# One more empty step between loading the spatial weights and using them, in a fused diffusion-transformer layer

## Chip, cores and metric

The kernel runs on one core of one Trainium2 chip. The time is device microseconds (us) of one execution; the median of several runs counts.

## The reference

One layer over 2048 latent tokens (model width 1024) and 256 context tokens, all in float32. The part that matters here is the token-mixing half: one combined input projection, whose columns are keys, values, queries, the gMLP's u and v, and two gates, then attention and the gMLP, merged by the gates.

```python
h_x = modulate(x, norm1_g[l], sh1, sc1)
p_x = h_x @ w_in[l]
...
q_x, u_x, vg_x, ga_x, gb_x = jnp.split(p_x[..., KV_COLS:], REST_SPLITS, axis=-1)
...
gm_x = gmlp_spatial(jax.nn.gelu(u_x), jax.nn.gelu(vg_x), gm_norm_g[l], gm_ws[l], gm_bs[l])

def gmlp_spatial(u, v, gm_norm_g, gm_ws, gm_bs):
    ...
    vg = rmsnorm(v.reshape(b, nc, CHUNK, GM_GROUPS, GM_GROUP_DIM), gm_norm_g)
    s = jnp.einsum('gpq,bnqgc->bnpgc', gm_ws, vg) + gm_bs.T[:, :, None]
    return u * s.reshape(b, n, GM_WIDTH)
```

So for each chunk of 128 tokens and each of 8 groups of 64 channels, a 128x128 matrix (the spatial weights) mixes the tokens of the chunk. Attention, the merge with the output projection, and a squared-ReLU MLP of width 4096 follow.

## The kernel before

The kernel works in stages: the projection (in the profile from 0 to about 700 us), attention (to about 1380), the merge (to about 1760), and the MLP. Products in float32 are made from three products of split operands (high and low parts, lines 1744 to 1746, or 186 to 188). The big products use seven products p of half blocks in place of eight, in the order SUMS = 0, 1, 5, 6, 4, 2, 3.

**The projection** (`project`, line 1112) goes over two blocks of 1024 tokens (block 0 holds the token quarters b = 0 and 1, block 1 holds 2 and 3). Its columns come in two pairs and eight gate groups. Pair 0 gives keys, values and queries, pair 1 gives u and v. A pair runs in 14 steps of 24 matmuls (`pairs_run`), a gate group in seven steps p of 12 matmuls (`Gate.step`), written below as gate step (group, p). Block 0 runs pair 0, groups 0 and 1, pair 1, groups 2 to 7. Block 1 runs pair 0, pair 1, then all the groups, where one group's last steps alternate with the next group's first ones. Three steps of group 7 of block 0 are left over and run among the first ones of block 1.

**The jobs.** What must be done with the pairs' results beside these products is written as jobs, Python generators cut into parts by `yield`, in one list, first in first out: keys and queries work of each quarter, the preparation of the next block's rows (`h_ahead`, 20 parts), and `mixing(b, c)`, the gMLP of quarter b and half c of the groups. There are eight mixing jobs, here called (b, c). A tick takes the next part of the job at the head of the list:

```python
763          for _ in range(n):
764              while self.work and (self.busy or not self.hold):
765                  self.busy = True
766                  if next(self.work[0], self) is not self:
767                      break
768                  self.work.pop(0)
769                  self.busy = False
```

A job that is done makes room for the next in the same tick. In a pair there are two ticks a step, one for each 12 matmuls (lines 751 and 760). In the gates there is one tick after each step, but in block 1 two, from the sixth step on:

```python
1107              groups[g].step(p)
1108              self.tick(1 + (both and at > 4))
```

**A mixing job** has 12 parts: 1 loads v, u and the norm weights; 2 and 3 are the gelu of v; 4 its norm; 5 and 6 the gelu of u; 7 multiplies by the norm; 8 splits v (`split`, line 157 on the vector engine DVE); 9 loads the spatial weights `ws` (512 KB from DRAM, line 919, on SP's queue); 10 and 11 do the products (`mm3`, lines 186 to 188: six matmuls of 256 columns for each of two pairs of groups) and line 929 on DVE; 12 transposes the result and stores it in `gm_d` (lines 937 to 947). Its large tiles come from tag m (`m4`), which has four slots; h_ahead's rows, the queries, the copies of block 1's rows at the change of blocks (`raw_loaded`, from `h_d`), and the outputs of groups 6 and 7 in block 1 use the same four.

Where the ticks fall: job (0,0) starts in pair 1 of block 0 and its load is written in gate step (3,1), its products in (2,2) and (3,5). h_ahead follows until gate step (5,3), then job (0,1), of which five parts are written until gate step (7,1). There all that is left of h_ahead and of the job in hand is written out in one go (lines 1233 to 1236), and block 1's first rows are loaded and split. Jobs (1,0) and (1,1) wait until the sums for the operands of block 1 are written (step p = 6 of pair 0), whatever came before, and run along the pairs. Then come keys and queries of quarters 2 and 3, then (2,0), (2,1), (3,0) and (3,1) along the gates of block 1: (2,0) starts in gate step (1,5), with two ticks a step; its load is in (1,4), its products in (2,1). (3,1) has its load in (3,3), its products in (4,6), and ends in (5,0). After gate step (5,6) whatever is left in the list would be run out (lines 1221 to 1223); nothing is left there.

**The order on each engine.** The program is written in that order, but outside of some ranges (the opening and the later stages, which `order` pins) the build's planner orders the instructions of each engine itself: it takes the one written first among those whose operands it reckons to be there. So the place where a part is written is its priority, not its place in the engine's queue. Each engine then runs its queue in order and waits at the head. Tiles with the same tag keep the order in which they are written.

Of the kernel before, what the change touches and what calls it, by code (L numbers as in the profile page):

```python
# [50 lines left out]
def f32(ap):  # L51
    return ap.bitcast(F32)
# [20 lines left out]
class Kern:  # L73
# [818 lines left out]
    def mixing(self, b, c):  # L892
        nc = self.nc
        v, u = (self.raw_values(b, j, c) for j in range(2))
        gn = self.t2([256])
        nc.sync.dma_start(
            gn,
            self.I["gm_norm_g"].rearrange("o g d -> o (g d)").partition_broadcast(P)[
                :, 0, c * 256 : (c + 1) * 256
            ],  # L900
        )
        yield
        for _ in self.gelu2(v):
            yield
        (rb,) = self.heads_rstd([v], 4.0 / HD, 16 * EPS)
        yield
        for _ in self.gelu2(u):
            yield
        nc.vector.tensor_tensor(out=v, in0=v, in1=rb, op=ALU.mult)
        gc = (  # L910
            gn.rearrange("p (g d) -> p g d", d=HD).unsqueeze(1).broadcast_to([P, TT, 4, HD])
        )
        nc.vector.tensor_tensor(out=v, in0=v, in1=gc, op=ALU.mult)
        yield
        vh, vl = self.m4([TT, 4, HD], F32R), self.m4([TT, 4, HD], F32R)
        self.split(v, vh, vl, lo_eng="dve")
        yield
        ws = self.m4([2, 4, P], F32R)
        nc.sync.dma_start(f32(ws).rearrange("p n g q -> p n (g q)"), self.ws_d[c])
        yield  # L920
        for g0 in (0, 2):
            ps = self.bank([2, TT, HD])
            for g in (g0, g0 + 1):
                self.mm3(
                    ps[:, g - g0], ws[:, 0, g], ws[:, 1, g],
                    vh[:, :, g, :], vl[:, :, g, :], True, True,
                )
            for g in (g0, g0 + 1):
                nc.vector.scalar_tensor_tensor(
                    out=u[:, :, g, :], in0=ps[:, g - g0],  # L930
                    scalar=self.gbs[:, c * 4 + g : c * 4 + g + 1], in1=u[:, :, g, :],
                    op0=ALU.add, op1=ALU.mult,
                )
            yield
        for f in range(2):
            ps = self.bank([TB])
            self.transposes(
                ps,
                [
                    u[:, t, 2 * f : 2 * f + 2].rearrange("p g d -> p (g d)")  # L940
                    for t in range(TT)
                ],
            )
            ot = self.t2([TB])
            nc.scalar.copy(ot, ps)
            lo = c * 256 + f * P
            nc.scalar.dma_start(self.gm_d[b][lo : lo + P, :], ot)
        yield
# [1486 lines left out]
```

## Time and profile before

| | us |
|---|---|
| median of 3 runs (lowest 3007.8) | 3008.2 |
| the profiled execution | 3012.1 |
| its span | 3010.1 |

| stretch of the span | us |
|---|---|
| projection until the first load of `ws` | 0 to 272 |
| projection from there on, all eight mixing products | 272 to 700 |
| attention, merge, MLP | 700 to 3010 |

The profile gives busy times of each engine (PE is the matrix engine, PEld its weight loads, DVE the vector, ACT the scalar engine, POOL GpSimd, SP the engine that issues most DMAs), what each engine waited for, and the chain of work that ended last. In a row, `m<-ws_d` reads "tile of tag m, from ws_d". A bracket at the end of a row of the order of time is idle time of the engine before it, and what ended it.

### The profile page before, as it was taken

The page shows a single profiled execution, that of the slowest core. Times are in us where ns is not written, and L with a number is a line of the kernel's source. Part 1 is how long each engine was busy: PE and PEld are TensorE (multiplying, and loading weights), DVE is VectorE, ACT ScalarE, POOL GpSimd, SP SyncE. Part 2 cuts the span into 40 slices and gives each one's busy share as a digit, 9 for nine tenths or more (in the row PEclk, how much of TensorE's full clock was granted, in tenths as well). Part 3 has the DMA queues.
Part 4 walks back from the last instruction along what each step waited for, and adds up shares of the span by engine and source line. Part 5 has one row for each costly group of instructions (what it writes and reads, how often), then busy time and mean ns, then how long its engine had stood idle before and what let it go on. Part 6 is the DMA issues. An engine that isn't in the chain of part 4 may idle for free.

```text
span 3010.1 us, 37936 instructions
## 1 busy us (share of the span) xinstructions
PE 2931.4 (97%) x13325; PEld 2210.1 (73%) x13325; DVE 2069.9 (69%) x2983; ACT 1418.8 (47%) x2318; POOL 650.8 (22%) x470
## 2 busy tenths in 40 slices
PE   7899999999999999999999989999999999999999
PEld 5778788876455555556888878888887888888887
DVE  5857487766888887867555587776676766654555
ACT  5544865554454544444222354444454344444432
POOL 0000000001899898894212200000000000000000
PEclk9999999999999999999999999999999999999999
DMA  7687967774010010016776658888766544447554
GB/s 274 186 293 262 315 205 225 253 245 150 24 36 29 22 37 22 22 35 189 238 215 194 183 198 308 310 301 304 263 216 223 185 154 154 154 158 272 210 208 156
DMA packets 386175, 559.04 MB, mean 186 GB/s; under 512 B 38640, under 2 KB 192416, under 8 KB 385984
## 3 DMA queue, kind: packets, MB, share of 16 engines
q1 hardware_dynamic: 373616, 535.89, 53.7%
q10 hardware_dynamic: 12368, 20.73, 1.9%
q8 instruction: 105, 1.72, 0.2%
q14 instruction: 86, 0.70, 0.1%
HBM read 379.75 MB, written 176.69 MB: 185 GB/s over the span
## 4 chain that ended last, share of the span: by engine, by line
PE 82%; DMA 6%; DVE 6%; ACT 3%; issue 2%; SPq 1%; ACTq 0%; POOL 0%; DVEq 0%; POOLq 0%
PE b L1744 14%; PE b L1745 14%; PE b L1746 14%; PE b L2322 8%; PE b L2291 4%; PE b L2310 4%; PE b L186 4%; PE b L187 4%; PE b L188 4%; PE b L2246 3%; PE a L1744 2%; PE a L1746 2%; PE a L1745 2%; PE b L192 1%; DMA m<-ws_d 1%
## 5 line engine op out<-in xcount | busy, mean ns | idle before, releaser
L2257 DVE TENSOR_REDUCE ts<-b 128x1 f32<-128x512 f32 x492 | 302.0, 681 | 69.7 <-PE b L2246 69.7
L2342 POOL TENSOR_TENSOR ac<-ac,p 128x512 f32<-128x512 f32 x214 | 306.1, 1463 | 54.5 <-ACT p L2314 54.5
L1860 DVE TENSOR_TENSOR b<-b,b 128x1024 fp32r<-128x1024 f32 x170 | 200.7, 1221 | 137.1 <-ACT b L1859 136.3
L1859 ACT CAST b<-b 128x1024 fp32r<-128x1024 f32 x170 | 170.6, 1051 | 225.3 <-PE b L1746 100.1
L2314 ACT ACTIVATE p<-b 128x512 f32<-128x512 f32 x384 | 194.0, 624 | 175.5 <-PE b L2310 168.3
L1745 PE MATMUL b<-b,b 128*128 128x512 f32 x680 | 265.2, 390 | 3.6 <-DVE b L1860 3.5
L1744 PE MATMUL b<-b,b 128*128 128x512 f32 x680 | 266.2, 391 | 1.7 <-DVE f L1881 1.5
L1746 PE MATMUL b<-b,b 128*128 128x512 f32 x680 | 264.7, 389 | 0.0
L2342 POOL TENSOR_TENSOR ac<-p,p 128x512 f32<-128x512 f32 x32 | 51.5, 1629 | 746.1 <-DMA raw<-in_w_mod 736.8
L2342 POOL TENSOR_TENSOR ac<-ac,t 128x512 f32<-128x512 f32 x152 | 204.1, 1374 | 0.0
L2291 PE MATMUL b<-h,h 128*128 128x512 f32 x576 | 187.3, 405 | 3.3 <-ACT p L2314 2.2
L2322 PE MATMUL b<-p,h 128*64 128x512 f32 x768 | 187.3, 611 | 0.0
L2310 PE MATMUL b<-h,h 128*128 128x512 f32 x576 | 178.6, 391 | 0.0
L1745 PE MATMUL b<-hb,b 128*128 128x512 f32 x446 | 173.8, 390 | 0.0
L1754 DVE TENSOR_TENSOR f<-f,b 128x512 f32<-128x512 f32 x160 | 109.2, 682 | 78.4 <-issue 45.7
L1744 PE MATMUL b<-hb,b 128*128 128x512 f32 x415 | 161.9, 390 | 0.0
L1746 PE MATMUL b<-hb,b 128*128 128x512 f32 x415 | 161.3, 389 | 0.0
L1745 PEld LDWEIGHTS b<-b,b 128*128 128x128 f32 x680 | 127.6, 188 | 32.2 <-DVE b L1860 5.5
L2291 PEld LDWEIGHTS b<-h,h 128*128 128x128 f32 x576 | 103.6, 188 | 63.8 <-DVE ts L2257 24.3
L1744 PEld LDWEIGHTS b<-b,b 128*128 128x128 f32 x680 | 127.6, 188 | 29.9 <-ACT b L1859 2.8
L1746 PEld LDWEIGHTS b<-b,b 128*128 128x128 f32 x680 | 127.7, 188 | 26.5
L157 POOL TENSOR_TENSOR bw<-bw,bw 128x512 fp32r<-128x512 f32 x58 | 75.9, 1331 | 235.6 <-ACT bw L153 233.8
(440 smaller groups left out, 7243.0 us busy)
## 6 DMA issues: line engine op xcount, KB each, us to landing
ao_d<-f SPq DMA_DIRECT2D x224, 256.0 KB
f<-in_w_ff SPq DMA_DIRECT2D x48, 1024.0 KB
b<-ao_d SPq DMA_DIRECT2D x85, 512.0 KB
b<-w2o_d SPq DMA_DIRECT2D x85, 512.0 KB
w2o_d<-f SPq DMA_DIRECT2D x112, 256.0 KB
f<-in_w_in SPq DMA_DIRECT2D x38, 512.0 KB
f<-x_d SPq DMA_DIRECT2D x64, 256.0 KB
hb<-ao_d SPq DMA_DIRECT2D x54, 256.0 KB
```

Of the source, the lines that this page charges most:

```text
L186: mm(ps, sh, mh, start=start, stop=False)
L1744: mm(ps, wh, hh, start=start and k == 0, stop=False, skip_group_check=True)
L1745: mm(ps, wh, hl, start=False, stop=False, skip_group_check=True)
L1746: mm(ps, wl, hh, start=False, stop=k == len(w) - 1, skip_group_check=True)
L1859: nc.scalar.copy(h, f32(l))
L1860: nc.vector.tensor_tensor(out=l, in0=f32(l), in1=f32(h), op=ALU.subtract)
L2257: nc.vector.tensor_reduce(out=self.mx[:, t, h, c : c + 1], in_=ps[h], axis=AX.X, op=ALU.max)
L2291: self.nc.tensor.matmul(self.pts[j][h], k.KA[c][self.kv][:, ks], self.qa[h], start=True, stop=False, skip_group_check=True,)
L2310: self.nc.tensor.matmul(s, k.KB[c][self.kv][:, ks], self.qb[h], start=False, stop=True, skip_group_check=True,)
L2314: self.nc.scalar.activation(pt[h], s, AF.Exp)
L2322: nc.tensor.matmul(self.o[h * HD : (h + 1) * HD, :], k.V[c][:, i, self.kv * HD : (self.kv + 1) * HD], pt[h], start=j == 0, stop=j == NKT - 1,)
L2342: nc.gpsimd.tensor_tensor(out=self.acc[e][:, h], in0=old[:, h], in1=pt[h], op=ALU.add)
```

## The change

One more `yield` in `mixing`, behind the load of the spatial weights: the job gets a 13th part, an empty one, between the load and the products. No instruction is added or removed. It holds for all eight mixing jobs.

```diff
         yield
         ws = self.m4([2, 4, P], F32R)
         nc.sync.dma_start(f32(ws).rearrange("p n g q -> p n (g q)"), self.ws_d[c])
+        yield
         yield
         for g0 in (0, 2):
             ps = self.bank([2, TT, HD])
```

## The prediction

> **What bounds the kernel now.** I read the page first (busy times, chain), then the busy time of TensorE (PE) by stretch, then PE's waits by what ended them, then the order of time around the eight loads. Parts 1 and 4 of the page:
>
> ```profile
> span 3010.1 us, 37936 instructions
> ...
> PE 2931.4 (97%) x13325; PEld 2210.1 (73%) x13325; DVE 2069.9 (69%) x2983; ACT 1418.8 (47%) x2318; POOL 650.8 (22%) x470
> ...
> PE 82%; DMA 6%; DVE 6%; ACT 3%; issue 2%; SPq 1%; ACTq 0%; POOL 0%; DVEq 0%; POOLq 0%
> PE b L1744 14%; PE b L1745 14%; PE b L1746 14%; PE b L2322 8%; PE b L2291 4%; PE b L2310 4%; PE b L186 4%; PE b L187 4%; PE b L188 4%; PE b L2246 3%; PE a L1744 2%; PE a L1746 2%; PE a L1745 2%; PE b L192 1%; DMA m<-ws_d 1%
> ```
>
> PE is the bound. The load that the change is about (m<-ws_d) has 1% of the chain, but a share of the chain is no gain: while the load is under way PE works on other products. What counts is PE's idle time where the changed jobs lie. Busy time by stretch (columns: stretch, its length, PE busy, weight load, DVE, ACT, POOL, granted clock, DMA share, GB/s):
>
> ```profile
> 272.00:383.00 111.00, 108.11 (x512) 88.10 (x512) 55.85 (x103) 78.48 (x121) 0.00 (x0) 1.00 0.89 306
> 383.00:403.00 20.00, 16.04 (x84) 13.29 (x83) 12.78 (x20) 9.68 (x15) 0.00 (x0) 1.00 0.93 311
> 403.00:655.00 252.00, 245.77 (x1218) 211.03 (x1217) 189.55 (x350) 148.67 (x243) 0.00 (x0) 1.00 0.69 224
> 655.00:700.00 45.00, 39.98 (x180) 31.24 (x178) 20.91 (x41) 22.57 (x39) 0.00 (x0) 0.96 0.73 240
> ```
>
> The first load of the spatial weights is issued at 272, and the projection is over at about 700. PE's idle time there is 2.9 + 4.0 + 6.2 + 5.0 = 18.1 us, 0.6% of the span. This bounds what any better order of the jobs can bring. It lies thickest at the change of blocks (383 to 403) and at the end (655 to 700). From PE's waits, and from those of SP's queue (columns: total, times, longest):
>
> ```profile
> PE b L186 <- DMA m<-ws_d: 5.8, 6, 1.4
> SPq L919 <- DVE m L157: 20.2, 7, 7.5
> ```
>
> Six of the eight jobs make PE wait for these weights, 5.8 us in all. That is the only cost that the change aims at.
>
> **The change, part by part.** It adds no instruction, no DMA and no wait. Each of eight mixing jobs gets a 13th part, an empty one, between part 9 (the load) and what was part 10 (six products of 256 columns and two DVE operations). All that it can do is to move where instructions are written. How much PE work one step is, I take from the order of time in the gates:
>
> ```profile
> 656.70 0.39 PE L1744 MATMUL a<-h,f 128*128 128x512 f32 x1
> ...
> 658.52 0.39 PE L1746 MATMUL a<-h,f 128*128 128x512 f32 x1
> ```
>
> Nine matmuls in a row, so (658.52 - 656.70) / 8 = 0.228 us each, and a gate step of 12 is 2.7 us. In the pairs a tick also has 12 matmuls.
>
> *The distance from load to use.* By the ticks in the code: job (0,0) has one step of 12 matmuls between load and products and gets two. Job (0,1) is written out in one go at the change of blocks, none before and after. Jobs (1,0) and (1,1) run along the pairs, one tick each: one step becomes two. Jobs (2,0) to (3,1) run in the gates of block 1 with two ticks a step. There the empty part shares a step with a neighbour: one product block stands between load and use before, and one after, for all four. So only three of eight loads get more distance as written, and (0,0) has no wait to lose.
>
> *Does the written distance decide?* Rows of the last job, (3,1), and of (1,0) and (1,1):
>
> ```profile
> 452.65 0.39 PE L186 MATMUL b<-m,m 128*128 128x256 f32 x1 [1.06 <-DMA m<-ws_d]
> ...
> 484.01 0.39 PE L186 MATMUL b<-m,m 128*128 128x256 f32 x1 [0.61 <-DMA m<-ws_d]
> ...
> 673.51 0.38 SPq L919 DMA_DIRECT2D m<-ws_d  x1
> ...
> 675.89 0.50 PE L1744 MATMUL a<-hx,e 128*128 128x512 f32 x1 [0.84 <-DVE t L2187]
> ...
> 678.68 0.38 PE L186 MATMUL b<-m,m 128*128 128x256 f32 x1 [1.13 <-DMA m<-ws_d]
> 680.29 0.59 ACT L2177 COPY m<-a 128x512 f32<-128x512 f32 x1 [3.79 <-PE b L187]
> ...
> 684.99 0.59 ACT L2177 COPY m<-b 128x512 f32<-128x512 f32 x1 [2.09 <-PE b L1746]
> ```
>
> The products of job (3,1) are written in gate step (4,6). Yet the products with the late-loaded gate weights (hx,e, a step p = 2 of group 5, written eleven steps later) stand before them on PE. So the build's planner had already moved these products back, to where it reckoned the load done. Counted in the program before, the PE instructions written after a job's products but standing ahead of them are 0, 72, 46, 26, 43, 74, 100 and 114 for the eight jobs. The 12 or so that the empty part adds as written are fewer than all but the first of these. So I expect the products to stay where the planner reckons the load landed, and PE to run into the load as before. Saving: between 0 and the whole 5.8; of it 1.06 + 0.61 = 1.7 is in the two jobs whose distance grows. I take 0, because the lags (26 and more) are nearer to "decided by the reckoned landing" than to "decided by the place written".
>
> The Trainium skill, DMA: Bandwidth & Descriptors, section Rules for kernel authors, says to issue a DMA early, compute, and wait late, so that its fixed cost overlaps. By that rule the six waits go, and the sum below has -5.8 in place of 0 and ends at -3.1 (rival G). The trace agrees that the waits are there, and no row shows them gone.
>
> *What is set back: the change of blocks.* Job (0,0) ends one tick later, so the preparation of the next block's rows (h_ahead) starts and ends one gate step later, and job (0,1) behind it too. This chain ends in PE's first products of block 1, through the shared slots of tag m:
>
> ```profile
> 391.91 2.26 SPq L552 DMA_DIRECT2D m<-h_d  x3
> ...
> 393.85 7.52 DMA m<-h_d
> ...
> 394.81 0.40 PE L1746 MATMUL b<-hx,t 128*128 128x512 f32 x1
> ...
> 396.08 0.62 ACT L572 CAST h<-m 128x512 fp32r<-128x512 f32 x1 [1.56 <-DMA m<-h_d]
> ...
> 396.75 0.45 PE L1744 MATMUL a<-f,h 128*128 128x384 f32 x1 [1.54 <-ACT h L572]
> ```
>
> Block 0's rows are loaded back into m slots that job (0,1) frees; cast by ACT, then PE starts after 1.54 us idle. PE has nothing left to put there: the three steps left of group 7 (the last ends with the matmul at 394.81) are already done by then. So a chain later by one step costs 2.7 us. Bounds: 0, if job (0,1) catches up; 2.7 plus a slow start of PE (1.6, below), 4.3. I take 2.7: counted as above, the first loads of h_ahead stand on SP without any lag, so a later tick is a later start.
>
> *What is set back: block 1.* (1,0) and (1,1) end two ticks later in sum. The keys and queries jobs follow, and (2,0) starts two ticks later, one gate step, 2.7 us. Behind it the four mixing jobs are not paced by ticks:
>
> ```profile
> 590.25 5.37 DMA m<-ws_d
> ...
> 673.51 5.12 DMA m<-ws_d
> ```
>
> First and last of four loads on the chain: (673.51 - 590.25) / 3 = 27.8 us a job, while 12 ticks are six steps, 16.4 us. They are paced by their own chain (slots of m, loads of 7 us, gelu, normalisation), which the empty part does not lengthen. So the last job ends 2.7 us later. Groups 6 and 7 copy their first product into m slots that this job frees (the copy at 680.29 starts right behind its products). Cover: the first product of group 7, 12 matmuls, 2.7 us, now done after them (its copy is at 684.99), can go ahead. I take 0; if that cover fails, 2.7, and 4.3 with a slow start. No job is left over for the place where the rest is run out, after step (5,6): the last part falls in step (4,2) instead of (5,0), three steps short of it.
>
> *A slow start of PE*, the extra price of a longer stall:
>
> ```profile
> 661.29 0.50 PE L1744 MATMUL a<-h,t 128*128 128x512 f32 x1 [2.38 <-ACT a L2182]
> ...
> 662.37 0.63 PE L1744 MATMUL a<-h,t 128*128 128x512 f32 x1
> 662.80 0.63 PE L1745 MATMUL a<-h,t 128*128 128x512 f32 x1
> ...
> 664.93 0.50 PE L1744 MATMUL a<-h,t 128*128 128x512 f32 x1
> ```
>
> After 2.38 us of idle the matmuls come up to 0.43 us apart instead of 0.228: the tenth starts at 664.93, so nine steps take 3.64 us where 9 x 0.228 = 2.05 would do, 1.6 us lost. The granted clock of 655 to 700 is 0.96. A stall of 1.54 + 2.7 at the change of blocks would be longer than that one. I count the 1.6 in the upper bounds only: the forecast's stall may well come in two parts, and the 1.54 us of now stand in a stretch with the full clock (1.00).
>
> The Trainium skill, TensorE: Matmul & The Clock Gate, section HAM oscillation, tells of such a loss after idle gaps over about 3.4 us; it speaks against the change, and the sum would be +4.3 by it, inside the forecast's own spread. This trace shows the loss behind a shorter gap.
>
> **Sum.** Waits for the weights 0, change of blocks +2.7, end of the projection 0: +2.7 us. The profiled execution took 3012.1 us (span 3010.1) and would take 3014.8. The median of the runs is 3008.2, 0.13% below it, and there it gives 3010.9. All later stages (from 700 on) follow the projection unchanged.
>
> **The rivals.**
> *The waits go (G).* The products are placed later on PE and the load is hidden: down to 3008.2 - 5.8 = 3002.4, or 3006.5 for the two jobs alone. For it: six waits of at most 1.44 us are less than one step. Against it: the lags.
> *Nothing moves (N).* The planner takes up the empty step wholly and the order is as before: 3008.2. For it: no instruction is added, and lags of up to 114. Against it: h_ahead starts without lag.
> *The chain of block 1 grows (L).* If each of its four jobs does get one step longer and PE ends with the last job: 4 x 2.7 + 2.7 = 13.5, 3021.7. For it: PE already idles 11% of the time from 655 to 700 (5.0 of 45 us). Against it: no product block is added there.
> *Slower by over 2% (S).* One mechanism: SP issues its queue in order, and everything behind a spatial-weights load waits with it. Its longest wait there is 7.5 us. If each of the eight jobs were set back by that much on the path, 8 x 7.5 = 60 us, 3068. It decides from 7.5 us a job upwards. Against it: the mean is 20.2 / 7 = 2.9, and PE was busy meanwhile.
>
> **How the numbers follow.** The forecast (3008.5 to 3016.8, the upper end with no cover and both slow starts: 2 x (2.7 + 1.6) = 8.6) has 0.45, G 0.25, N 0.15, L 0.12, S 0.02, and 0.01 is left for a faster time that no row explains. The time is the forecast's, 3010.9. The range takes in G to its end and L: 3001 to 3024, with some 2 us beyond L and 1 beyond G for the scatter of runs (3007.8 to 3008.2, profiled 3012.1). About 2%, 60 us, is what a measurement of this kernel can tell from no change; all of PE's idle time in reach is 18.1, so faster is 0.01, the same 0.97, slower 0.02.
>
> **What would show it.** Right: the waits of L186 on m<-ws_d stay at 4 us or more in sum; PE's idle time from 383 to 403 grows by 2 to 5 us; the four loads of block 1 stay some 28 us apart; PE's busy time stays at 2931. Wrong: if the waits for m<-ws_d fall to 1 us or less (the written place does decide); if the idle time at the change of blocks does not grow (job (0,1) catches up); if the products of job (3,1) come over 5 us later against the end of the projection (block 1's chain grew).

## The result, and the profile after

| | before | after |
|---|---|---|
| median of the runs, same chip (us) | 3006.35 | 3013.11 |
| ratio with its 95% interval | | 1.0022 [1.0012, 1.0032] |
| profiled execution, its span (us) | 3012.1, 3010.1 | 3018.1, 3016.3 |

The change makes the kernel slower by 6.6 us (0.0022 x 3008; 3.6 to 9.6 by the interval). Among the eleven runs of the kernel before is one of 3643.2 us, which moves its median by less than 0.5. The forecast was +2.7: the range held the time and the sign was right, but the loss is more than twice as large as the sum said, and, as the profile shows, it comes from other places.

From the page of the changed kernel, its parts 1 and 4:

```profile
span 3016.3 us, 37943 instructions
...
PE 2931.2 (97%) x13325; PEld 2211.0 (73%) x13325; DVE 2068.0 (69%) x2983; ACT 1418.5 (47%) x2318; POOL 652.7 (22%) x470
...
PE 82%; DMA 6%; DVE 6%; ACT 3%; issue 2%; SPq 0%; POOL 0%; ACTq 0%; DVEq 0%; POOLq 0%
```

The work is the same: every engine has the same count of instructions, and PE the same busy time over the whole span to 0.2 us. Where PE stood still, is in the busy time by stretch of the changed kernel (columns as in the prediction):

```profile
272.00:383.00 111.00, 106.99 (x505) 86.59 (x503) 53.93 (x103) 77.71 (x119) 0.00 (x0) 1.00 0.88 301
383.00:403.00 20.00, 16.23 (x84) 13.29 (x83) 13.05 (x20) 9.14 (x14) 0.00 (x0) 1.00 0.88 300
403.00:655.00 252.00, 241.85 (x1175) 206.92 (x1174) 187.19 (x345) 143.93 (x238) 0.00 (x0) 0.99 0.67 216
655.00:700.00 45.00, 36.66 (x167) 29.19 (x165) 20.91 (x39) 20.05 (x34) 0.00 (x0) 0.89 0.73 238
```

PE's idle time (length less busy) against before: 4.0 instead of 2.9, 3.8 instead of 4.0, 10.2 instead of 6.2, 8.3 instead of 5.0. The change of blocks (383 to 403), where the prediction put its whole cost, has not grown. The added idle time is in block 1 (403 to 700), 7.2 us, and a little, 1.1, before the change of blocks.

The same view cut at events rather than at times says more: from the first load of `ws` to the last product of the projection, and from there to the last product of attention. Before, and after:

```profile
272.00:734.00 462.00, 442.52 (x2130) 365.76 (x2130) 310.00 (x563) 269.17 (x436) 0.00 (x0) 1.00 0.74 242
734.00:1385.57 651.57, 643.98 (x2970) 335.10 (x2968) 532.12 (x677) 325.91 (x660) 574.20 (x406) 0.99 0.11 35
```

```profile
272.00:746.40 474.40, 446.95 (x2130) 368.17 (x2129) 310.62 (x564) 268.58 (x436) 0.00 (x0) 0.98 0.72 236
746.40:1392.30 645.90, 639.66 (x2970) 333.85 (x2968) 528.27 (x674) 325.57 (x660) 576.08 (x406) 1.00 0.12 35
```

Both stretches together: 1113.57 us with 1086.50 busy before, 1120.30 with 1086.61 after. The length grows by 6.7, the idle time by 6.6 (27.1 to 33.7), the busy time by 0.1. But in that sum two things cancel. The projection's stretch is 12.4 us longer: 8.0 of idle time, and 4.4 of busy time for the same 2130 matmuls, which ran slower (granted clock 0.98 in place of 1.00). Attention is 5.7 shorter, 4.3 of it busy time (granted clock 1.00 in place of 0.99). Over the fourteen traces of this document attention takes some 641 to 652 us, and the trace of the kernel before is at the upper end; that the change shortens it is not shown. So idle time alone is not the loss: PE also loses time in the matmuls behind its stalls.

What PE waited for between 300 and 720 us. Before (only the row that the prediction does not show; the other is m<-ws_d with 5.8), and after:

```profile
PE a L1744 <- ACT a L2182: 5.1, 4, 2.4
```

```profile
PE a L1745 <- ACT a L2183: 14.2, 4, 7.5
PE b L186 <- DMA m<-ws_d: 2.5, 4, 1.1
...
PE b L186 <- ACT b L2194: 1.4, 1, 1.4
...
PE b L192 <- ACT m L528: 1.0, 1, 1.0
```

(Behind the added line all line numbers are one higher: L2182 before is L2183 after.) The waits that the change aims at did shrink, from 5.8 to 2.5. But another wait grew by 9.1: L2183 is `nc.scalar.copy(ps, self.u[:, 0])` in `Gate.step` at p = 1. There ACT first takes the tanh of the sum in PSUM, then copies a saved sum back into the same bank, and the products of the next step (p = 5, a<-h,t) add to it. PE cannot go on until that copy is done. The longest such wait, 7.5 us, in the order of time on PE:

```profile
665.00 0.39 PE L1747 MATMUL a<-h,f 128*128 128x512 f32 x1
...
667.75 0.39 PE L1747 MATMUL a<-hx,e 128*128 128x512 f32 x1
675.66 0.80 PE L1745 MATMUL a<-h,t 128*128 128x512 f32 x1 [7.52 <-ACT a L2183]
676.25 0.63 PE L1746 MATMUL a<-h,t 128*128 128x512 f32 x1
...
680.95 0.58 PE L1745 MATMUL a<-hx,t 128*128 128x512 f32 x1
681.36 0.39 PE L1746 MATMUL a<-hx,t 128*128 128x512 f32 x1
```

The same place on ACT, before and then after. L882 and L886 are the gelu of job (3,1), L2173 (L2174) the gate's tanh, L2182 (L2183) the copy:

```profile
654.18 0.60 ACT L2173 ACTIVATE t<-a 128x512 f32<-128x512 f32 x1 [0.30 <-PE a L1746]
656.67 1.15 ACT L882 ACTIVATE t<-m 128x512 f32<-128x512 f32 x2 [1.89 <-DMA m<-p_d]
...
660.12 0.63 ACT L882 ACTIVATE t<-m 128x512 f32<-128x512 f32 x1
660.66 0.58 ACT L2182 COPY a<-t 128x512 f32<-128x512 f32 x1
```

```profile
668.44 0.63 ACT L882 ACTIVATE t<-m 128x512 f32<-128x512 f32 x1 [2.32 <-DMA m<-p_d]
...
670.99 0.63 ACT L882 ACTIVATE t<-m 128x512 f32<-128x512 f32 x1 [0.53 <-DMA m<-p_d]
...
672.56 0.58 ACT L2174 ACTIVATE t<-a 128x512 f32<-128x512 f32 x1
...
674.51 0.62 ACT L886 ACTIVATE t<-t 128x512 f32<-128x512 f32 x1
675.02 0.58 ACT L2183 COPY a<-t 128x512 f32<-128x512 f32 x1
```

Before, the gate's tanh started right when its sum was there, and only the copy stood among the gelu. After, the sum was there at 665.4 at the latest (the last product a<-h,f ahead of the stall is the row at 665.00), but tanh and copy stand in ACT's queue behind a gelu whose operands are still on their way: ACT idles 2.32 us for the load m<-p_d, which the gate does not need, and PE waits for ACT. The Trainium skill, PSUM — Partial Sum Buffer, section Engine vs sequencer instructions, states that the ScalarE queue is strictly first in, first out; the trace agrees: the tanh runs 7.2 us after its operand (672.56 - 665.39), though ACT stood idle within that time.

That the gate jobs lie elsewhere is seen on SP's queue, before and then after. L842 is the first load of the queries of quarter 2 and L804 loads the keys of quarter 3, both for jobs that stand ahead of (2,0) in the list; L2129 (L2130) are stores of pair 1's sums, most of which wait for DVE; L871 is (2,0)'s own first load:

```profile
497.36 0.42 SPq L842 DMA_DIRECT2D m<-p_d  x1
...
524.37 0.37 SPq L804 DMA_DIRECT2D t<-p_d  x1
529.11 4.77 SPq L2129 DMA_DIRECT2D p_d<-t  x4
...
566.91 0.92 SPq L871 DMA_DIRECT2D m<-p_d  x2
```

```profile
504.08 0.42 SPq L842 DMA_DIRECT2D m<-p_d  x1
...
530.33 6.12 SPq L2130 DMA_DIRECT2D p_d<-t  x4
536.55 0.39 SPq L804 DMA_DIRECT2D t<-p_d  x1
...
573.76 0.37 SPq L871 DMA_DIRECT2D m<-p_d  x1
...
602.41 0.32 SPq L919 DMA_DIRECT2D m<-ws_d  x1
...
684.26 0.38 SPq L919 DMA_DIRECT2D m<-ws_d  x1
```

The load of `ws` for (2,0) is 12.2 us later (602.41 against 590.25); the prediction had 2.7 for that. The keys load, written later because (1,0) and (1,1) end two ticks later, is 12.2 later too (536.55 - 524.37) and now stands behind four more stores. But the rows do not show that the stores hold it. The queries loads ahead of it are 6.7 us later already. And ACT's copy L866, one of the last of that queries job, runs until 536.64; in a kernel described below (e6) the trace lists the keys load as waiting for that copy:

```profile
536.06 0.58 ACT L866 COPY t<-b 128x512 f32<-128x512 f32 x1
```

```profile
SPq L804 <- ACT t L866: 0.8, 1, 0.8
```

Nor is the delay handed on unchanged: (2,0)'s first load is 6.9 us later (573.76 against 566.91), so some of the 12.2 is made up for by then, and the rest of the delay of its `ws` arises within the job. What set each part of it was not settled.

### The profile page after: what moved, and what is told of

Read it like the earlier page. It is cut to its first block, busy times and chain, and to the rows that moved or that the text cites. A ratio compares the mean times of both kernels' runs of the same rounds, so it can differ in the third digit from the quotient of the medians.

```text
span 3016.3 us, 37943 instructions
## 1 busy us (share of the span) xinstructions
PE 2931.2 (97%) x13325; PEld 2211.0 (73%) x13325; DVE 2068.0 (69%) x2983; ACT 1418.5 (47%) x2318; POOL 652.7 (22%) x470
## 4 chain that ended last, share of the span: by engine, by line
PE 82%; DMA 6%; DVE 6%; ACT 3%; issue 2%; SPq 0%; POOL 0%; ACTq 0%; DVEq 0%; POOLq 0%
PE b L1745 14%; PE b L1746 14%; PE b L1747 14%; PE b L2323 8%; PE b L2292 4%; PE b L186 4%; PE b L187 4%; PE b L188 4%; PE b L2311 4%; PE a L1745 3%; PE b L2247 3%; PE a L1746 3%; PE a L1747 3%; PE b L192 1%; DMA f<-in_w_in 1%
## 5 line engine op out<-in xcount | busy, mean ns | idle before, releaser
L1745 PEld LDWEIGHTS b<-b,b 128*128 128x128 f32 x680 | 127.6, 188 | 29.5 <-ACT b L1860 2.3
L1758 ACT ACTIVATE f<-f 128x512 f32<-128x512 f32 x96 | 60.5, 630 | 141.8 <-DVE f L1755 141.8
```

What stands on the lines that cost most here:

```text
L1745: mm(ps, wh, hh, start=start and k == 0, stop=False, skip_group_check=True)
```

## The experiments

Twelve kernels ran, those sent together on one chip beside the kernel before. The table has what the text below reads from them: the ratio; PE's idle time from 272 to 740 us (468 less its busy time there); the longest wait of PE behind the gate's copy; how much later than before (2,0)'s `ws` is loaded, counted from the first load of `ws` (318.3 us in the kernel before, 590.25 - 271.97); and how many of pair 1's last eight stores still follow the keys load of quarter 3 on SP.

| kernel | ratio | idle | copy wait | (2,0) later by | stores behind the keys load |
|---|---|---|---|---|---|
| before | 1 | 20.9 | 2.4 | 0 | 4 |
| after | 1.0022 [1.0012, 1.0032] | 27.5 | 7.5 | 12.1 | 0 |
| e1_block0 | 0.9996 [0.9984, 1.0007] | 23.2 | 2.4 | 4.0 | 4 |
| e2_pairs | 1.0016 [1.0003, 1.0028] | 22.5 | 6.6 | 8.6 | 0 |
| e3_gates | 1.0002 [0.9991, 1.0014] | 19.3 | 1.7 | 0.9 | 4 |
| e4_end | 1.0030 [1.0019, 1.0042] | 29.5 | 5.9 | 18.1 | 0 |
| e5_merge | 0.9998 [0.9988, 1.0008] | 22.3 | 2.5 | 1.2 | 4 |
| e6_one_tick | 1.0014 [1.0005, 1.0024] | 24.7 | 4.7 | 4.5 | 2 |
| e7_last_job_after | 0.9998 [0.9985, 1.0011] | 23.1 | 2.5 | 12.6 | 0 |
| e8_last_job_before | 0.9985 [0.9974, 0.9996] | 18.5 | 2.4 | 2.4 | 4 |
| e9_later | 1.0024 [1.0015, 1.0033] | 27.3 | 2.2 | 11.5 | 0 |
| e10_earlier | 1.0010 [1.0001, 1.0019] | 22.9 | 1.1 | 5.6 | 4 |
| e11_start_back | 1.0027 [1.0017, 1.0037] | 26.3 | 2.1 | 7.8 | 2 |
| e12_block1 | 1.0005 [0.9994, 1.0016] | 21.5 | 1.6 | 4.1 | 2 |

**Which of the eight jobs costs it** (e1 to e3). The empty step is kept in two jobs of block 0 (e1), in (1,0) and (1,1) along the pairs (e2), or in the four gate jobs (e3):

```diff
         yield
-        yield
+        if b == 0:
+            yield
```

with `b == 1` in e2 and `b >= 2` in e3.

> The empty step in jobs (0,0) and (0,1) alone. If the loss comes at the change of blocks (the step of the prediction), this one carries it: some 3 to 7 us over the kernel before, with more idle time of PE between 370 and 405 us. If the loss comes from ACT's queue in the gates of block 1 (PE waiting up to 7.5 us for a gate's copy that stands behind job (3,1)'s gelu), the jobs of block 1 start at a tick that this edit does not move, and the time is that of the kernel before within 2 us, the longest wait for that copy staying near 2.4 us.

> The empty step in jobs (1,0) and (1,1) alone: their waits for the spatial weights may go (1.7 us at most), and every later job of block 1 is written two ticks, one gate step, later. If a later start of the gate jobs alone makes the long wait behind job (3,1), this one is 4 to 8 us slower than before and shows a wait of PE of 5 us or more for the copy of line 2182 or its like. If it needs the empty steps inside the gate jobs, the time stays within 2 us of before.

> The empty step in jobs (2,0) to (3,1) alone, which start where they did. If the place of the gate jobs against the gates' own copies in ACT's queue is the cause, this one shows the long wait (5 us or more) and 4 to 8 us more than before; if the cause is a later start (two ticks from the earlier jobs), it stays within 2 us of before. The waits for the spatial weights should stay in the gates, since the distance as written is one product block as before.

Block 0's two steps alone cost nothing that can be measured (-1.2 us, -4.8 to +2.1), nor do those in the gate jobs (+0.6). The two in the pair jobs cost 4.8 (0.9 to 8.4) and bring the long wait by themselves, in the same place:

```profile
670.34 0.79 PE L1746 MATMUL a<-h,t 128*128 128x512 f32 x1 [6.61 <-ACT a L2184]
```

So the prediction's place (block 0's jobs, change of blocks) falls.

**The distance or the later end?** (e4, e5). In e4 the empty step stands at the end of the job: 13 parts, but no more distance from load to products. In e5 it stands behind the load, and the `yield` between the multiplication by the norm and the split is taken out: more distance, 12 parts.

```diff
             nc.scalar.dma_start(self.gm_d[b][lo : lo + P, :], ot)
         yield
+        yield
```

```diff
         nc.vector.tensor_tensor(out=v, in0=v, in1=gc, op=ALU.mult)
-        yield
         vh, vl = self.m4([TT, 4, HD], F32R), self.m4([TT, 4, HD], F32R)
         ...
         nc.sync.dma_start(f32(ws).rearrange("p n g q -> p n (g q)"), self.ws_d[c])
         yield
+        yield
```

> The empty step at the end of every mixing job instead of behind its load: the same number of ticks, no more distance between load and products. If the ticks cost and the distance gains, this one is slower than the changed kernel by what the waits for the spatial weights lose there (5.8 to 2.5 us, so some 3 us), thus 8 to 11 us over before. If the distance does nothing, it equals the changed kernel, 5 to 8 us over before. If only the distance matters, it equals the kernel before.

> The empty step stays, and the step between the norm's multiplication and the split (parts 7 and 8) goes: every job again has 12 parts, so every later job is written where it was, and the load is written one tick earlier against its products. If the loss comes from the later start of the gate jobs, it is gone: the time is that of the kernel before, or up to 3 us less if some waits for the spatial weights go; the longest wait for the gate's copy is again near 2.4 us. If the distance itself costs, it stays 5 to 8 us slower.

The 13th part costs 9.0 us (5.7 to 12.6) without any distance, and the distance without a 13th part costs nothing (-0.6). It gains nothing either: in e5 PE's waits for `ws` are 8.6 us in sum, the longest 4.1, more than before. So it is the later end of the jobs that costs, and not the distance. Whether the distance gains something in the changed kernel stays open, as e4's 9.0 and its 6.6 do not differ by more than their intervals.

**One tick** (e6). The empty step is left only in job (1,1).

```diff
         yield
-        yield
+        if (b, c) == (1, 1):
+            yield
```

> The empty step in job (1,1) alone: job (2,0) starts one tick later, which is already the next gate step, (0,3), the same as with two ticks. If the gate step in which the gate jobs start decides, this one is as slow as the kernel with both pairs jobs changed: 3 to 7 us over before, with a wait of 5 us or more for the gate's copy. If each tick counts, the loss is half of that, 2 to 3 us, with a wait of some 4 us.

A single empty step in one of eight jobs costs 4.2 us (1.5 to 7.2) and brings a wait of 4.7 behind the copy. The time falls in the first of the two ranges expected, the wait with the second. On SP the keys load now stands behind two more of pair 1's stores.

**The gelu in ACT's way** (e7, e8). Job (3,1) leaves out the gelu of v and u, and takes the squares for its norm on DVE: its long work on ACT is gone. The rest is the changed kernel (e7) or the kernel before (e8).

```diff
-        for _ in self.gelu2(v):
+        for _ in self.gelu2(v, (b, c) == (3, 1)):
...
+            if skip:
+                yield
+                continue
...
+            if dve:
+                nc.vector.tensor_tensor(out=sq, in0=s, in1=s, op=ALU.mult)
```

> The changed kernel, with job (3,1) leaving out its gelu of v and u, and taking the squares of its norm on DVE in place of ACT: nothing of this job that waits for its loads stands on ACT before the split. If PE's long wait comes from ACT being held by this job's gelu, the wait of 7.5 us for the gate's copy falls under 2 us, and the time is no more than 3 us above that of the kernel before with the same edit, or below it. If the long wait has another cause, it stays over 5 us.

> The kernel before with the same edit (job (3,1) leaves out its gelu, squares of its norm on DVE): the base for the run with the changed kernel. Its wait of 2.4 us for the gate's copy should go to under 1 us, and with the slow matmuls behind it the time falls by 2 to 5 us against the kernel before.

The 7.5 us wait goes: from 600 to 740 us no wait of PE is above 1.2, and the longest copy waits left, 2.5, are at 307.8 and 594.7. So it was this job's work on ACT that held the copy. In e8 the time falls as expected (4.5 us), and the copy wait at job (3,1) is gone; the 2.4 in the table is another one, at 589.9 us. What remains of the change is 1.0013 between the two, with intervals of about 0.0012 on either side of each: neither nothing nor the whole 1.0022 can be excluded.

**Later, earlier, and back** (e9 to e11). In e9 (1,0) and (1,1) get two empty steps each, the other jobs none. In e10, the kernel before, and e11, the changed one, the keys jobs of quarters 2 and 3 lose one of the two `yield`s behind their load. By the count of written parts (2,0) starts one gate step earlier in e10, and in e11 where it started before the change.

```diff
         yield
-        yield
+        if b == 1:
+            yield
+            yield
```

```diff
             yield
-            yield
+            if b < 2:
+                yield
```

> Two empty steps in place of one, but only in the jobs (1,0) and (1,1): (2,0) starts two gate steps later than in the kernel before (four ticks), the other six jobs have 12 parts. Theory A (ACT takes its queue in order, and the gate step in which the gate jobs start decides whether a gate's tanh and copy stand ahead of job (3,1)'s gelu or behind it): the time is not proportional to the ticks. The stall of PE behind a gate's copy near 640 to 690 us is either as long as with one gate step (4.7 to 6.6 us, time 3011 to 3014) or gone (2.5 us or less, time within 2 us of before), depending on where the gelu falls; a growth beyond 7 us is not expected. Theory B (each step that the gate jobs start later costs its 2.7 us): the double of the run with the pair jobs alone, +5 of +10 us by its interval, 3014 to 3018.

> The kernel before, with one part fewer in the keys work of quarters 2 and 3: (2,0) starts one gate step earlier than in the kernel before, and the mixing jobs have their 12 parts. Theory A (order in ACT's queue): not faster as a rule; the longest wait of PE behind a gate's copy depends on where the gelu of (3,1) falls, 1 to 6 us, time 3005 to 3013. Theory B (each gate step costs 2.7 us): 2.7 us or more faster than before, 3003 to 3006.

> The changed kernel with 13 parts in all eight mixing jobs, and with one part fewer in the keys work of quarters 2 and 3, so that (2,0) starts in gate step (1,5) again, as in the kernel before. Theory A (the later start of the gate jobs brings the stall): the wait of PE behind a gate's copy at job (3,1) is 2.5 us or less again, and the time is within 2 us of before, 3007 to 3011; what is left is the 1 to 2 us near 306 to 393 us from block 0's jobs. Rival (the empty steps in the gate jobs themselves, or block 0, bring it): a copy wait of 5 us or more stays, and +5 us or more, 3012 to 3016.

With twice the empty steps of e2, e9 is 7.2 us above before (4.5 to 9.9), between the two theories. Its stalls have changed their name: the longest is 4.4 us behind another ACT operation of the gate (L2187, a sum copied out of PSUM), and 2.2 behind the copy. e10 speaks against B: written earlier by a step, it is 3.0 us slower (0.3 to 5.7).

e11 is the miss that counts. As expected the long wait is gone, and the time is as high as with the change. Its longest groups of waits from 300 to 720:

```profile
PE a L1746 <- ACT a L2184: 6.6, 5, 2.1
PE b L186 <- DMA m<-ws_d: 5.1, 7, 1.3
PE a L1746 <- ACT h L572: 1.8, 2, 1.5
PE a L1746 <- ACT t L2179: 1.7, 1, 1.7
```

No wait is above 2.1 us. The idle time is in many small ones, 26.3 us from 272 to 740. Theory A, that one wait behind one gelu is the cost, falls as the whole story: the wait is where the loss shows in the changed kernel, and without it the loss shows elsewhere. Nor did e10 and e11 move in time what was moved in writing. Their loads of `ws` for (2,0) are issued at 599.32 and 600.29 us. With their first loads of `ws` at 275.49 and 274.21 these are 5.6 and 7.8 us later than in the kernel before, where e10's was written a step earlier and e11's in the same step. So e11 speaks against the one wait, and not against the later start as the cause.

**The sum instead of the one wait** (e12). This kernel is e11 with the empty step only in block 1's six jobs. It tests what was left: that the time follows the sum of PE's waits, whichever they are.

```diff
-        yield
+        if b >= 1:
+            yield
```

> The run with the start put back, but with the empty step only in the six jobs of block 1 (b of 1 and more); block 0's two jobs have their 12 parts. Theory C (formed after the start put back took the long stall away, 7.5 to 1.7 us, and left the time at 1.0027: no single wait carries the cost, the time follows the sum of PE's waits between 265 and 740 us, by a straight line through the ten kernels with all the work so far 0.94 us for each us of it, zero at 20.0): PE's idle time from 272 to 383 falls from 4.8 us back to 2 to 3, the sum from 25.5 to some 23, the time to 1.0005 to 1.0015 of before; whatever the sum is, the time lies within 3 us of the line. Rival D (the empty step in the gate jobs itself costs it, or the two parts moved in the keys work): the time stays at 1.002 to 1.003 whatever the sum of the waits.

The ratio is 1.0005, +1.5 us. The sum of its listed waits is 20.9, lower than the 23 expected, and for it the line gives 0.94 x (20.9 - 20.0) = 0.8. The stretch from 272 to 740 in e11 and e12:

```profile
272.00:740.00 468.00, 441.75 (x2125) 363.06 (x2125) 309.60 (x562) 268.64 (x437) 0.00 (x0) 1.00 0.73 238
```

```profile
272.00:740.00 468.00, 446.47 (x2142) 367.72 (x2141) 310.14 (x564) 271.53 (x441) 0.00 (x0) 1.00 0.74 241
```

4.7 us less idle, and 6.6 us less time (0.0027 - 0.0005, the intervals just apart). Theory C holds here and D falls: the gate jobs and the keys work are the same in both. (C says where the time is, and not what puts it there.) Block 0's two steps, which cost nothing alone (e1), do cost in this company.

**What the runs say together.** Two columns of the table go with the time over the twelve kernels that do all the work (without e7 and e8). A straight line through idle time and ratio has 0.99 us of time for each us of idle and a correlation of 0.85; one through the delay of (2,0) has 0.59 us for each us later, a correlation of 0.88, and passes zero at 0.4 us. Single kernels lie up to 4 us off either, since a trace is one execution and a ratio many. The first says where the time is, the second what goes ahead of it: gate jobs that run later. And where they run later by 7.8 us or more without anything left out, the keys load stands behind all of pair 1's stores (or all but two, e11). But the two do not move in step: counted as in the table, the keys load is not later at all in e10, where (2,0)'s `ws` is 5.6 later, and 17.9 later in e9, where it is 11.5. Both groupings were made after the runs, and a kernel that moves this load alone was not tried: that the delay comes by way of SP's queue is not shown. No version beat the kernel before with all its work done. That its order is simply a good one, and that many another order costs some us by waits of its own, is a rival that these runs do not exclude.

## Why the prediction was right or wrong

**Right: the bound and the range.** PE's time in the projection was the right account: PE is busy 2931.2 us as said, and the stretch up to the projection's last product is 12.4 us longer, more than the whole loss. A ratio near 1 followed from that and came. That the sign came out as forecast is luck: the one term that carried it measured nothing, and the time went where the sum had 0.

**Wrong: "change of blocks +2.7".** This was the whole sum, and it measured -0.2 (idle 4.0 to 3.8). The set-back of h_ahead exists, but shows earlier: 1.1 us more idle from 272 to 383, of which 0.8 is a longer wait of PE for h_ahead's scaled rows (L528, 1.0 in place of 0.2). At 398 PE waits 0.58 for the cast of block 1's first rows, where it waited 1.54. The bound "0, if job (0,1) catches up" was the value to take, and e1 shows the two steps alone to cost nothing measurable.

**Wrong: "the end of the projection 0, with cover".** Here the time went: 7.2 us more idle from 403 to 700. Two steps of the reasoning failed. First the size of the shift: "one gate step, 2.7 us" took the written place for the time, although the same prediction had shown that written places and times differ by up to 114 instructions. The loads of `ws` shifted by 12.2 us for (2,0), and by 10.8 for (3,1) (684.26 against 673.51). Second, the search for a price looked only at slots of tag m and PE's cover. It did not ask who stands behind the late jobs on ACT, though the row with the answer was quoted: PE's 2.38 us of idle on "ACT a L2182" served only to price a slow start. That wait became the 7.5. (The later stages were held to follow unchanged; in the one trace of each kernel attention is 5.7 us shorter, within the spread of that stretch.)

**Half right: "waits for the weights 0".** They fell from 5.8 to 2.5, short of "4 or more" and far from gone. More distance is not what did it: with the step in the gate jobs alone (e3) and with distance alone (e5) the sums are 5.7 and 8.6. Rival G's gain did come in part and was paid back three times over behind the copy (+9.1). Why these waits shrink in the changed kernel was not settled.

**Right: the pace of block 1's chain.** (684.26 - 602.41) / 3 = 27.3 us a job, against 27.8: the chain did not grow longer a job, it was moved as a whole. The products of (3,1) start 10.5 us later (689.16 against 678.68) where the projection's end is 12.4 later, so they did not come later against it. Rival L falls. Rival S named SP's queue in order as a mechanism but put it at the eight loads of `ws`; its longest wait there is now 8.6 us in place of 7.5. The price is a tenth of S's.

**Mis-sized: the slow start.** It was counted in the upper bounds only. After the 7.5 us stall thirteen matmuls take 5.70 us (675.66 to 681.36) where 13 x 0.228 = 2.96 would do: 2.7 us more, in place of 1.6, and the granted clock of 655 to 700 is 0.89. Two shorter stalls of the changed kernel (2.75 us at 592.15, 1.93 at 647.03) have 1.7 each behind them. The three come to 6.1 where the kernel before has 1.6, and the difference is about the 4.4 us of busy time by which the projection's stretch grew. As PE counts as busy in slow matmuls, an account of idle time alone leaves it out.

## What to carry to other kernels

An empty step that adds nothing to do is still a change of every later job's place: on a kernel whose bound engine is 97% busy, what it can cost is the small waits that the old order happened to avoid, so look at all in-order queues that the moved jobs share with the bound engine's helpers, not only at the wait that the step aims at. When a work item that waits for a load goes into the queue of an engine that also frees or refills PSUM for the next product, the load's delay becomes the matrix engine's: ask what stands behind it. And before one long wait in a trace is called the cause, take it away: here the time stayed.

## What was not expected of the hardware

How long PE must stand still before it starts slowly is not one number here. Behind a wait of 1.93 us in the changed kernel the matmuls come 0.43 us apart, nearly twice the 0.228 of the usual pace; behind one of 2.34 us in e10 they come at the full pace:

```profile
647.03 0.67 PE L1745 MATMUL a<-h,t 128*128 128x512 f32 x1 [1.93 <-ACT a L2183]
647.50 0.63 PE L1746 MATMUL a<-h,t 128*128 128x512 f32 x1
647.92 0.63 PE L1747 MATMUL a<-h,t 128*128 128x512 f32 x1
```

```profile
545.87 0.50 PE L1745 MATMUL a<-f,hx 128*128 128x512 f32 x1 [2.34 <-ACT a L734]
546.21 0.40 PE L1746 MATMUL a<-f,hx 128*128 128x512 f32 x1
546.44 0.39 PE L1747 MATMUL a<-f,hx 128*128 128x512 f32 x1
```

The prediction took the loss behind a wait of 2.38 us as if each wait of that length had it. Behind the waits of 4.4 us and more that are named above it was there each time.

The median of the kernel before lay between 3006.1 and 3013.1 us in the five comparisons, a spread as wide as the effect: only ratios of runs taken side by side on one chip tell these kernels apart.
